# Two ties and a shorter step for the row products in a two-layer hybrid decoder trunk

## The chip, the cores and the metric

The kernel runs on one core of a Trainium2 chip. The metric is device time in microseconds (us), the median of three runs. TensorE (PE) multiplies matrices, VectorE (DVE) and ScalarE (ACT) work element by element, GpSimd (POOL) does a few tiny operations here, and the queue of SyncE (SP) issues the weight transfers.

## The reference

A sequence of 256 tokens of width 1024 passes two equal layers in fp32. In each layer `mod = silu(c) @ w_ada + b_ada` gives six vectors (shift, scale and gate of the mixer, shift, scale and gate of the MLP):

```
h = rms_norm(x, g_pre_mix) * (1 + sc_m) + sh_m
y = token_mixer(h)                 # MoBA and DSA attention, norms, out projection
x = x + gt_m * rms_norm(y, g_post_mix)
h = rms_norm(x, g_pre_ffn) * (1 + sc_f) + sh_f
a = causal_conv(h @ w_up_act)      # depthwise, width 3
y = (gelu(a) * (h @ w_up_lin)) @ w_down     # 2816 columns
x = x + gt_f * rms_norm(y, g_post_ffn)
```

## The kernel before

Tokens lie in two halves of 128 rows, t=0 and t=1. Each fp32 product is made of three fp32r products on PE: both operands are split into a high part, rounded, and a low part, the rest (`hh`/`hl` of activations, `wh`/`wl` or `dh`/`dl` of weights). A weight tile `raw` (1 MB, ring of 6 buffers, filled by the SP queue in program order) is split by `split`: ACT copies it to `wh` or `dh` (L141; L137 with a gain, in the out projection), DVE subtracts (L142, L138). `wh` and `wl` have rings of five buffers, `dh` and `dl` share a ring of six with other tiles.

The scale and gate vectors of the modulation are made on DVE: `gemv_v` multiplies a 128x1024 part of `w_ada` with the row `crow` and sums along it, one *row product* (L190), two per `raw` buffer. It is a generator: it runs beside the main work and yields, after each product, the number of steps after which it is traced again (`gap`). Columns 32 to 40 are the MLP scale, traced in attention with gap 9 in layer 0; columns 40 to 48 are the MLP gate, traced in the MLP loop from tile 3 (layer 0) or 7 (layer 1).

The program text gives each instruction a priority; a scheduler then sets the order of each engine's list from priorities, dependencies and its own estimates, so an instruction may move away from the place in which it was traced. `tc.issue_after(x)` ties an instruction: in the list it comes behind `x`. On the chip each engine works its list off.

The stages that the change touches, in order of time:

- Attention of layer 0: projections (L400), scores and value products (L420), masks and maxima of the scores on DVE (L484), exps on ACT (L488), scaling (L496), transposes (L503), copied by ACT (L505).
- Out projection (L576 to L578, `mm3`), then the *boundary*: residual (L319, L327), sums of squares on ACT (L255), the root on POOL (L263, L265), `norm_T` (L287: two tensor_scalar per half of the rows, then eight PE transposes, L275), and `mod_T`, which applies scale and shift and splits the result into `hh` and `hl` (L298, L306, L308 on ACT, L301, L310 on DVE).
- `lin`: the linear branch of the first four MLP tiles as one projection (L400) into banks b0 (t=0) and b1 (t=1). Its eight weight blocks k lie in four units; the units of k=0 to 5 are split into `dh`/`dl`, the last one (k=6, 7) into `wh`/`wl`. The first half of its result is copied (L940), transposed (L275) and copied again (L934).
- MLP: 22 column tiles; `up(i)` multiplies (L576 to L578, `hh` with `wh`), then conv on ACT and DVE (L968, L969, L971), gelu on ACT (L973), product with the linear branch (L974), and the split of the result into `ah` (L975, ACT) and `al` (L976, DVE); `down` multiplies these with `dh`/`dl` of `w_down` three tiles later (L576 to L578 with `dh`; its second product is the first that reads `al`).

Of the kernel before, what the change touches and what calls it, by code (L numbers as in the profile page):

```python
# [74 lines left out]
def trunk(ctx: ExitStack, tc, plan, x, c, stream, small, rope, out):  # L75
# [29 lines left out]

    st = {"off": 0, "behind": ()}

# [16 lines left out]
    def split(raw, where=None, pin=False, gain=None):  # L124
# [7 lines left out]
        with ExitStack() as behind:  # L132
            for ins in st["behind"]:
                behind.enter_context(tc.issue_after(ins))
            put = tc.keep_in_program_order if pin else lambda ins: ins
            if gain is not None:
                put(nc.scalar.activation(out=hi[:, :n], in_=raw, func=AF.Copy, scale=gain))  # L137
                put(nc.vector.scalar_tensor_tensor(out=lo[:, :n], in0=raw, scalar=gain, in1=hi[:, :n].bitcast(F32),  # L138
                                                   op0=OP.mult, op1=OP.subtract))
                return hi, lo  # L140
            put(nc.scalar.activation(out=hi[:, :n], in_=raw, func=AF.Copy))  # L141
            put(nc.vector.tensor_tensor(out=lo[:, :n], in0=raw, in1=hi[:, :n].bitcast(F32), op=OP.subtract))  # L142
        return hi, lo
# [39 lines left out]
    def gemv_v(l, j0, j1, gap, behind=None):  # L183

        for j in range(j0, j1, 2):
            r = load(("v_a", l, j, 2048))[0]
            for i in range(2):
                ri = r[:, 1024 * i:1024 * i + 1024]
                with tc.issue_after(behind) if behind else ExitStack():
                    nc.vector.scalar_tensor_tensor(out=ri, in0=ri, scalar=1.0, in1=crow, op0=OP.mult, op1=OP.mult,  # L190
# [93 lines left out]
    def norm_T(t, r, banks):  # L284
        xn = [t2(), t2()]
        for h in range(2):
            nc.vector.tensor_scalar(out=xn[h], in0=xt[:, t, 512 * h:512 * h + 512], scalar1=r, scalar2=None,  # L287
                                    op0=OP.mult)
        return [turn4(xn[h], banks[h]) for h in range(2)]
# [497 lines left out]
    for l in range(DEPTH):  # L787
# [83 lines left out]
        if l == 0:  # L871
            bg.add("sf", gemv_v(l, 32, 40, 9))
        run_project("dq", qk_done(dqT, True, "D", 10))
# [32 lines left out]
        while st["out"] < 2:  # L906
# [3 lines left out]
        out_load(4, 8)  # L910
        first = [[split(raw, "lin" if g < 1 or u < 1 else None) for u, raw in enumerate(load(*us))]
                 for g, us in enumerate(project_units(l, "lin"))]
        raws = []
# [73 lines left out]
        for i in range(NF):  # L987
            if i == 3 + 4 * l:
                bg.add("ada", gemv_v(l, 40, 48, 4))
                bg.add("ada", gate_rows(l, "ffn"))  # L990
# [97 lines left out]
```

## Time and profile before

| | us |
|---|---|
| median of three runs | 683.57 (683.51 to 684.01) |
| profiled execution | 685.16 |
| its span, first to last instruction | 683.4 |
| PE busy | 664.3 (97%) |
| DVE busy | 551.2 (81%) |
| ACT busy | 423.9 (62%) |
| POOL busy | 27.7 (4%) |
| mean granted clock of PE | 0.995 |

The profiled execution is one run, 1.6 us above the median; differences are read from it and set against the median. A busy share is a mean over stages; idle time of PE is what a change can win or lose, and idle time of the other engines counts where PE waits for them.

### The profile page before, as it was taken

The numbers are of one execution on the slowest core, as the hardware profiler recorded it, in microseconds if no ns is written. First come the engines' busy times: TensorE is split into PE (matmuls) and PEld (weight loads), VectorE is DVE, ScalarE is ACT, GpSimd is POOL, SyncE is SP. The second block draws the span as 40 slices with busy tenths as digits, with TensorE's granted clock in tenths as the row PEclk, the third lists the DMA queues.
The fourth block names the chain that finished last, engine by engine and source line by source line (L and its number), as shares of the span: only waits on it lengthen the run. The fifth ranks groups of instructions, "written<-read, shape, count | busy, mean of one in ns | idle before, by whom it ended". The sixth has DMA issues, their size and how long they took to land.

```text
span 683.4 us, 11282 instructions
## 1 busy us (share of the span) xinstructions
PE 664.3 (97%) x4309; PEld 570.0 (83%) x4309; DVE 551.2 (81%) x1090; ACT 423.9 (62%) x788; POOL 27.7 (4%) x56
## 2 busy tenths in 40 slices
PE   8999899998999999999999999999999999999996
PEld 5877677776999999999988776877799999999994
DVE  6899999977999999897689995677689976666553
ACT  6566686977855555555586548778595555555441
POOL 1000000102000000000020000001200000000001
PEclk9999999999999999999999999999999999999999
DMA  9999649953599999896537642446146885555001
GB/s 358 421 413 395 220 192 368 340 188 124 211 361 351 396 371 346 327 335 244 186 124 267 256 165 83 147 161 240 70 185 245 313 304 195 208 185 186 0 1 62
DMA packets 24806, 163.04 MB, mean 239 GB/s; under 512 B 3344, under 2 KB 3760, under 8 KB 6576
## 3 DMA queue, kind: packets, MB, share of 16 engines
q1 hardware_dynamic: 23472, 159.77, 62.0%
q0 software_dynamic: 704, 2.11, 1.1%
q8 instruction: 34, 0.56, 0.3%
q10 hardware_dynamic: 576, 0.43, 0.2%
q14 instruction: 20, 0.16, 0.1%
HBM read 161.24 MB, written 1.06 MB: 238 GB/s over the span
## 4 chain that ended last, share of the span: by engine, by line
PE 78%; DVE 10%; ACT 5%; issue 3%; DMA 2%; POOL 1%; POOLq 0%; DVEq 0%; ACTq 0%
PE b L578 18%; PE b L577 18%; PE b L576 18%; PE b L400 14%; DVE wl L142 3%; PE b L420 3%; DMA raw<-in_stream_dram 2%; DVE iscore L443 2%; PE b L503 2%; DVE raw L709 1%; ACT t L255 1%; PE b L377 1%; PE b L275 1%; ACT wh L137 1%; ACT t L488 1%
## 5 line engine op out<-in xcount | busy, mean ns | idle before, releaser
L142 DVE TENSOR_TENSOR wl<-raw,wh 128x1024 fp32r<-128x1024 f32 (+1 forms) x146 | 173.0, 1195 | 31.6 <-ACT wh L141 28.6
L141 ACT ACTIVATE wh<-raw 128x1024 fp32r<-128x1024 f32 (+1 forms) x146 | 149.2, 1045 | 52.3 <-PE b L578 37.6
L576 PE MATMUL b<-hh,wh 128*128 128x256 f32 x640 | 180.0, 281 | 0.0
L578 PE MATMUL b<-hl,wh 128*128 128x256 f32 x640 | 179.7, 281 | 0.0
L577 PE MATMUL b<-hh,wl 128*128 128x256 f32 x640 | 179.6, 281 | 0.0
L577 PEld LDWEIGHTS b<-hh,wl 128*128 128x128 f32 x640 | 122.5, 191 | 1.3
L576 PEld LDWEIGHTS b<-hh,wh 128*128 128x128 f32 x640 | 120.2, 188 | 1.4
L578 PEld LDWEIGHTS b<-hl,wh 128*128 128x128 f32 x640 | 120.1, 188 | 0.0
L190 DVE SCALAR_TENSOR_TENSOR raw<-raw,crow 128x1024 f32<-128x1024 f32 x72 | 86.6, 1216 | 0.8 <-DMA raw<-in_stream_dram 0.7
L400 PE MATMUL b<-wh,hh 128*128 128x512 f32 (+1 forms) x184 | 73.7, 402 | 0.2
L400 PE MATMUL b<-wh,hl 128*128 128x512 f32 (+1 forms) x184 | 69.2, 391 | 0.0
L142 DVE TENSOR_TENSOR dl<-raw,dh 128x1024 fp32r<-128x1024 f32 (+2 forms) x47 | 56.8, 1210 | 12.6 <-ACT dh L141 12.6
L141 ACT ACTIVATE dh<-raw 128x1024 fp32r<-128x1024 f32 (+2 forms) x47 | 49.5, 1058 | 26.6 <-PE b L577 26.6
L968 ACT ACTIVATE t<-b,smt 128x256 f32<-128x256 f32 x44 | 25.1, 571 | 57.3 <-PE b L578 57.3
L576 PE MATMUL b<-dh,t 128*128 128x512 f32 x152 | 59.7, 393 | 0.0
L577 PE MATMUL b<-dh,t 128*128 128x512 f32 x152 | 59.6, 392 | 0.0
L578 PE MATMUL b<-dl,t 128*128 128x512 f32 x152 | 59.1, 389 | 0.0
L400 PE MATMUL b<-wl,hh 128*128 128x512 f32 (+1 forms) x184 | 55.0, 392 | 0.0
L400 PEld LDWEIGHTS b<-wh,hh 128*128 128x128 f32 x184 | 34.8, 189 | 8.5 <-issue 1.5
L400 PEld LDWEIGHTS b<-wl,hh 128*128 128x128 f32 x184 | 34.3, 191 | 6.0 <-issue 0.2
L400 PEld LDWEIGHTS b<-wh,hl 128*128 128x128 f32 x184 | 34.0, 189 | 6.0 <-issue 0.5
L969 DVE SCALAR_TENSOR_TENSOR t<-b,smt,t 128x255 f32<-128x255 f32 x44 | 21.1, 480 | 21.0 <-ACT t L968 20.8
(172 smaller groups left out, 1101.5 us busy)
## 6 DMA issues: line engine op xcount, KB each, us to landing
raw<-in_stream_dram SPq DMA_DIRECT2D x142, 1024.0 KB, 6.5
raw<-in_stream_dram SPq DMA_DIRECT2D x7, 804.0 KB, 11.4
gate<-gated POOLq DMA_DIRECT2D x4, 512.0 KB, 8.7
raw<-in_stream_dram SPq DMA_DIRECT2D x3, 512.0 KB, 6.3
xt<-in_x_dram SPq DMA_DIRECT2D x2, 512.0 KB, 4.1
raw<-in_stream_dram SPq DMA_DIRECT2D x1, 984.0 KB, 5.0
out_dram<-xt SPq DMA_DIRECT2D x2, 256.0 KB, 2.1
raw<-in_stream_dram SPq DMA_DIRECT2D x1, 328.0 KB, 5.5
```

Source lines behind the costliest of these rows:

```text
L141: put(nc.scalar.activation(out=hi[:, :n], in_=raw, func=AF.Copy))
L142: put(nc.vector.tensor_tensor(out=lo[:, :n], in0=raw, in1=hi[:, :n].bitcast(F32), op=OP.subtract))
L190: nc.vector.scalar_tensor_tensor(out=ri, in0=ri, scalar=1.0, in1=crow, op0=OP.mult, op1=OP.mult, accum_out=mods[l][:, j + i:j + i + 1])
L400: mm = lambda l_, k, i, start=False, stop=False: nc.tensor.matmul(a[:, :n], lhsT=l_[:, k, tt], rhs=w[k][i], start=start, stop=stop)
L420: ins = nc.tensor.matmul(out, lhsT=lhsT, rhs=rhs, **flags)
L443: nc.vector.scalar_tensor_tensor(out=sc, in0=r[:, j * nk:j * nk + nk], scalar=wi[:, h:h + 1], in1=fill[:, 256 - nk:] if first else sc, op0 ...
L503: nc.tensor.transpose(tp[:, 128 * j:128 * j + 128], e[:, 128 * j:128 * j + 128], ident)
L576: nc.tensor.matmul(y, lhsT=hh, rhs=wh, start=first, stop=False)
L577: nc.tensor.matmul(y, lhsT=hl, rhs=wh, start=False, stop=False)
L578: nc.tensor.matmul(y, lhsT=hh, rhs=wl, start=False, stop=last)
L968: nc.scalar.activation(out=z, in_=p[:, :256], func=AF.Identity, scale=w2[:, i:i + 1], bias=bc[:, i:i + 1])
L969: nc.vector.scalar_tensor_tensor(out=z[:, 1:], in0=p[:, :255], scalar=w1[:, i:i + 1], in1=z[:, 1:], op0=OP.mult, op1=OP.add)
```

## The change

Three edits. The row products of columns 32 to 40 are traced in layer 0 with gap 6, not 9. In layer 0 the split of lin's last unit (k=6, 7) is no longer made with the other units; it is put on a list, and `norm_T` of t=1 makes it, tied behind its second tensor_scalar. The gate products (columns 40 to 48, both layers) are each tied behind the lo split that was traced last. The number of instructions on each engine stays.

```
@@ -103,7 +103,7 @@
         return wrk.tile([128, n], F32, name=f"tiny{n}", tag=f"tiny{n}", bufs=8)
 
 
-    st = {"off": 0, "behind": ()}
+    st = {"off": 0, "behind": (), "then": []}
 
     def load(*units, cut=None):
 
@@ -139,7 +139,8 @@
                                                    op0=OP.mult, op1=OP.subtract))
                 return hi, lo
             put(nc.scalar.activation(out=hi[:, :n], in_=raw, func=AF.Copy))
-            put(nc.vector.tensor_tensor(out=lo[:, :n], in0=raw, in1=hi[:, :n].bitcast(F32), op=OP.subtract))
+            d = put(nc.vector.tensor_tensor(out=lo[:, :n], in0=raw, in1=hi[:, :n].bitcast(F32), op=OP.subtract))
+            st["lo"] = d.ins
         return hi, lo
 
 
@@ -186,7 +187,8 @@
             r = load(("v_a", l, j, 2048))[0]
             for i in range(2):
                 ri = r[:, 1024 * i:1024 * i + 1024]
-                with tc.issue_after(behind) if behind else ExitStack():
+                after = st["lo"] if behind == "lo" else behind
+                with tc.issue_after(after) if after else ExitStack():
                     nc.vector.scalar_tensor_tensor(out=ri, in0=ri, scalar=1.0, in1=crow, op0=OP.mult, op1=OP.mult,
                                                    accum_out=mods[l][:, j + i:j + i + 1])
                 yield gap
@@ -284,8 +286,11 @@
     def norm_T(t, r, banks):
         xn = [t2(), t2()]
         for h in range(2):
-            nc.vector.tensor_scalar(out=xn[h], in0=xt[:, t, 512 * h:512 * h + 512], scalar1=r, scalar2=None,
-                                    op0=OP.mult)
+            d = nc.vector.tensor_scalar(out=xn[h], in0=xt[:, t, 512 * h:512 * h + 512], scalar1=r, scalar2=None,
+                                        op0=OP.mult)
+        if t and st["then"]:
+            with tc.issue_after(d.ins):
+                st["then"].pop()()
         return [turn4(xn[h], banks[h]) for h in range(2)]
 
     def mod_T(p, t, scale, bias, hh, hl, between=None):
@@ -869,7 +874,7 @@
         bg.add("att", attend(mqT, mkT, mv, None, 0, oh, ol, ready[0]))
         dqT, dkT, dv = big("qT"), big("kT"), big("v")
         if l == 0:
-            bg.add("sf", gemv_v(l, 32, 40, 9))
+            bg.add("sf", gemv_v(l, 32, 40, 6))
         run_project("dq", qk_done(dqT, True, "D", 10))
         run_project("dk", qk_done(dkT, False, "D", 7))
         bg.add("att", attend(dqT, dkT, dv, masks, 4, oh, ol, ready[1]))
@@ -908,8 +913,14 @@
         bg.run(out_first(range(3)))
         bg.drain("att", "out")
         out_load(4, 8)
-        first = [[split(raw, "lin" if g < 1 or u < 1 else None) for u, raw in enumerate(load(*us))]
-                 for g, us in enumerate(project_units(l, "lin"))]
+        first = [load(*us) for us in project_units(l, "lin")]
+        first[0] = [split(raw, "lin") for raw in first[0]]
+        first[1][0] = split(first[1][0], "lin")
+        if l:
+            first[1][1] = split(first[1][1])
+        else:
+
+            st["then"].append(lambda: first[1].append(split(first[1].pop())))
         raws = []
         bg.run(out_last(range(3, 8)))
         bg.drain("sf")
@@ -986,7 +997,7 @@
 
         for i in range(NF):
             if i == 3 + 4 * l:
-                bg.add("ada", gemv_v(l, 40, 48, 4))
+                bg.add("ada", gemv_v(l, 40, 48, 4, "lo"))
                 bg.add("ada", gate_rows(l, "ffn"))
                 if l + 1 < DEPTH:
                     bg.add("ada", gemv_v(l + 1, 0, 32, 5))
```

Line numbers of the new kernel are higher: L190 becomes L192, L275 L277, L287 L289, L301 L306, L310 L315, L327 L332, L400 L405, L420 L425, L484 L489, L488 L493, L496 L501, L505 L510, L569 L574, L576 to L578 L581 to L583, L940 L945, L969, L971, L974, L976 become L980, L982, L985, L987.

What moves in the lists is shown at three places; the number behind a name tells buffers apart. First PE in layer 0's boundary, from the last `hh` products of lin's t=0 half on; `b0` is the bank of t=0, `b1` that of t=1, `b6` and `b4` take the transposes of t=1. Before:

```order
L400 MATMUL b0_1882<-wh_1694,hh_1762 128x512
L400 MATMUL b0_1882<-wl_1695,hh_1762 128x512
L400 MATMUL b0_1882<-dh_1680,hl_1763 128x512 x2
L400 MATMUL b0_1882<-dh_1684,hl_1763 128x512
L275 MATMUL b6_1849<-ident_75,t2_1845 128x128 x4
L275 MATMUL b4_1854<-ident_75,t2_1846 128x128 x4
L400 MATMUL b0_1882<-dh_1684,hl_1763 128x512
L400 MATMUL b0_1882<-dh_1690,hl_1763 128x512 x2
L400 MATMUL b0_1882<-wh_1694,hl_1763 128x512 x2
L400 MATMUL b1_1909<-dh_1680,hh_1762 128x512
```

Now:

```order
L405 MATMUL b0_1882<-dh_1692,hh_1758 128x512
L405 MATMUL b0_1882<-dl_1693,hh_1758 128x512
L405 MATMUL b0_1882<-wh_1845,hh_1758 128x512
L277 MATMUL b6_1849<-ident_75,t2_1841 128x128 x4
L277 MATMUL b4_1854<-ident_75,t2_1842 128x128 x4
L405 MATMUL b1_1909<-dh_1684,hh_1758 128x512
L405 MATMUL b1_1909<-dl_1685,hh_1758 128x512
L405 MATMUL b1_1909<-dh_1684,hh_1758 128x512
L405 MATMUL b0_1882<-wl_1846,hh_1758 128x512
L405 MATMUL b0_1882<-wh_1845,hh_1758 128x512
L405 MATMUL b0_1882<-wl_1846,hh_1758 128x512
```

The pair of the last unit (`wh_1694`, `wl_1695` before, `wh_1845`, `wl_1846` now) keeps one product ahead of the transposes; its other three, and the `hl` products, stand behind the transposes and behind three products of t=1.

Next DVE at the first MLP tile of layer 0, from the sixth split on; `t2_1987` is tile 0's conv result, `t2_1988` holds its `ah` and `al`. Before:

```order
L142 TENSOR_TENSOR dl_2072<-raw_2039,dh_2071 128x1024
L969 SCALAR_TENSOR_TENSOR t2_1987<-b5_1943,smt_71,t2_1987 128x255
L971 SCALAR_TENSOR_TENSOR t2_1987<-b5_1943,smt_71,t2_1987 128x254
L142 TENSOR_TENSOR wl_2098<-raw_2041,wh_2097 128x1024
L974 TENSOR_TENSOR t2_1987<-lin_1880,t2_1987 128x256
L142 TENSOR_TENSOR wl_2162<-raw_2155,wh_2161 128x1024
L976 TENSOR_TENSOR t2_1988<-t2_1987,t2_1988 128x256
```

Now:

```order
L142 TENSOR_TENSOR dl_2072<-raw_2039,dh_2071 128x1024
L142 TENSOR_TENSOR wl_2098<-raw_2041,wh_2097 128x1024
L192 SCALAR_TENSOR_TENSOR raw_2107,mod0_98<-raw_2107,crow_107 128x1024
L980 SCALAR_TENSOR_TENSOR t2_1987<-b5_1943,smt_71,t2_1987 128x255
L142 TENSOR_TENSOR wl_2162<-raw_2155,wh_2161 128x1024
L982 SCALAR_TENSOR_TENSOR t2_1987<-b5_1943,smt_71,t2_1987 128x254
L142 TENSOR_TENSOR wl_2193<-raw_2155,wh_2192 128x1024
L985 TENSOR_TENSOR t2_1987<-lin_1880,t2_1987 128x256
L142 TENSOR_TENSOR wl_2251<-raw_2157,wh_2250 128x1024
L987 TENSOR_TENSOR t2_1988<-t2_1987,t2_1988 128x256
```

A row product (of a buffer whose two products stood in the boundary before) and two more splits, `wl_2193` and `wl_2251`, stand ahead of tile 0's last operation. On ACT `wh_2192` and `wh_2250` stand ahead of tile 0's gelu now; before, the gelu was ahead of both.

Last ACT in attention, behind the exps (L488) of the first group of heads; the copies `t2_1422`, `t2_1432` (now `t2_1426`, `t2_1436`) are what the value products read. Before:

```order
L488 ACTIVATE t2_1392,tiny4_1397<-t2_1392,tiny4_1391 128x128 x4
L137 ACTIVATE wh_1503<-raw_1497,smt_71 128x1024
L137 ACTIVATE wh_1602<-raw_1600,smt_71 128x1024
L505 ACTIVATE t2_1422<-b7_1417 128x512
L137 ACTIVATE wh_1606<-raw_1600,smt_71 128x1024
L505 ACTIVATE t2_1432<-b6_1427 128x512
```

Now:

```order
L493 ACTIVATE t2_1396,tiny4_1401<-t2_1396,tiny4_1395 128x128 x4
L137 ACTIVATE wh_1507<-raw_1501,smt_71 128x1024
L137 ACTIVATE wh_1607<-raw_1605,smt_71 128x1024
L137 ACTIVATE wh_1611<-raw_1605,smt_71 128x1024
L510 ACTIVATE t2_1426<-b7_1421 128x512
L510 ACTIVATE t2_1436<-b6_1431 128x512
```

The third `wh` split went ahead of the first copy.

## Rows read from the trace of the kernel before

In the rows of the timeline the columns are: start in us, duration in us, engine, line, operation, out<-in, partitions x elements and type, count; in brackets the idle time ahead and who ended it.

**Rows 1.** The page's first part: busy time, share of the span and number of instructions of each engine.

```profile
PE 664.3 (97%) x4309; PEld 570.0 (83%) x4309; DVE 551.2 (81%) x1090; ACT 423.9 (62%) x788; POOL 27.7 (4%) x56
```

**Rows 2.** Timeline of PE in layer 0's boundary, from the last out product to the first up product.

```profile
157.44 0.40 PE L578 MATMUL b<-wl,hh 128*128 128x512 f32 x1
158.65 1.09 PE L275 MATMUL b<-ident,t 128*128 128x128 f32 x8 [0.81 <-DVE t L287]
159.85 0.50 PE L400 MATMUL b<-dh,hh 128*128 128x512 f32 x1
...
163.73 0.40 PE L400 MATMUL b<-wl,hh 128*128 128x512 f32 x1
...
164.43 0.85 PE L400 MATMUL b<-dh,hl 128*128 128x512 f32 x3
165.61 1.11 PE L275 MATMUL b<-ident,t 128*128 128x128 f32 x8 [0.32 <-DVE t L287]
166.48 0.94 PE L400 MATMUL b<-dh,hl 128*128 128x512 f32 x3
...
173.68 0.28 PE L576 MATMUL b<-hh,wh 128*128 128x256 f32 x1
```

**Rows 3.** Timeline of DVE in the same stretch.

```profile
154.09 1.22 DVE L190 SCALAR_TENSOR_TENSOR raw<-raw,crow 128x1024 f32<-128x1024 f32 x1
...
155.24 1.22 DVE L190 SCALAR_TENSOR_TENSOR raw<-raw,crow 128x1024 f32<-128x1024 f32 x1
...
156.99 1.21 DVE L142 TENSOR_TENSOR wl<-raw,wh 128x1024 fp32r<-128x1024 f32 x1
158.12 0.87 DVE L287 TENSOR_SCALAR t<-xt,tiny 128x512 f32<-128x512 f32 x2
...
165.06 0.88 DVE L287 TENSOR_SCALAR t<-xt,tiny 128x512 f32<-128x512 f32 x2 [0.97 <-POOL tiny L265]
```

**Rows 4.** Timeline of PE in layer 1's boundary, from the last out product to the transposes of t=1.

```profile
487.48 0.40 PE L578 MATMUL b<-wl,hh 128*128 128x512 f32 x1
487.71 1.19 PE L275 MATMUL b<-ident,t 128*128 128x128 f32 x8
489.00 0.50 PE L400 MATMUL b<-dh,hh 128*128 128x512 f32 x1
...
494.76 1.11 PE L275 MATMUL b<-ident,t 128*128 128x128 f32 x8 [0.34 <-DVE t L287]
```

**Rows 5.** Timeline of DVE in the same stretch of layer 1: the split that stands between the two tensor_scalar of t=0.

```profile
486.57 1.22 DVE L142 TENSOR_TENSOR wl<-raw,wh 128x1024 fp32r<-128x1024 f32 x1
```

**Rows 6.** Timelines at the first MLP tile of layer 0: DVE from the end of the six splits to `al` of tile 0, then the first two down products of PE.

```profile
178.30 0.48 DVE L969 SCALAR_TENSOR_TENSOR t<-b,smt,t 128x255 f32<-128x255 f32 x1
178.81 0.48 DVE L971 SCALAR_TENSOR_TENSOR t<-b,smt,t 128x254 f32<-128x254 f32 x1
179.21 1.22 DVE L142 TENSOR_TENSOR wl<-raw,wh 128x1024 fp32r<-128x1024 f32 x1
180.34 0.42 DVE L974 TENSOR_TENSOR t<-lin,t 128x256 f32<-128x256 f32 x1
...
181.81 0.42 DVE L976 TENSOR_TENSOR t<-t,t 128x256 fp32r<-128x256 f32 x1
...
182.60 0.40 PE L576 MATMUL b<-dh,t 128*128 128x512 f32 x1
182.83 0.40 PE L577 MATMUL b<-dh,t 128*128 128x512 f32 x1
```

**Rows 7.** Timelines in layer 0's attention: DVE, then ACT, then PE.

```profile
114.27 1.21 DVE L142 TENSOR_TENSOR wl<-raw,wh 128x1024 fp32r<-128x1024 f32 x1
115.40 0.68 DVE L569 TENSOR_TENSOR o<-o,b 128x512 f32<-128x512 f32 x1
...
120.32 0.28 DVE L484 CUSTOM_DVE_ANT_0 t<-b,mask 128x128 f32<-128x128 f32 x1
...
122.34 0.18 DVE L491 RECIPROCAL rs<-tiny 128x4 f32<-128x4 f32 x1 [0.24 <-ACT t L488]
...
120.67 0.38 ACT L488 ACTIVATE t<-t,tiny 128x128 f32<-128x128 f32 x1
...
123.76 2.17 ACT L137 ACTIVATE wh<-raw,smt 128x1024 fp32r<-128x1024 f32 x2
...
127.35 0.57 ACT L505 ACTIVATE t<-b 128x512 f32<-128x512 f32 x1
...
116.73 0.39 PE L400 MATMUL b<-wl,hh 128*128 128x512 f32 x1
...
127.98 1.09 PE L420 MATMUL b<-t,v 128*64 128x128 f32 x16 [0.20 <-ACT t L505]
```

**Rows 8.** Busy time by stretch: from and to, length, then PE, PEld, DVE, ACT and POOL with the number of instructions, granted clock of PE, DMA share and GB/s.

```profile
80.00:83.00 3.00, 1.81 (x11) 1.15 (x12) 3.00 (x15) 2.24 (x11) 0.00 (x0) 0.96 0.20 33
83.00:86.00 3.00, 3.00 (x12) 2.60 (x11) 3.00 (x11) 1.56 (x3) 0.00 (x0) 0.50 0.80 314
...
158.00:161.00 3.00, 2.24 (x13) 1.83 (x14) 2.81 (x8) 2.21 (x7) 1.06 (x2) 1.00 0.98 358
161.00:164.00 3.00, 2.50 (x12) 1.71 (x11) 2.67 (x5) 2.99 (x9) 0.00 (x0) 1.00 0.70 276
164.00:167.00 3.00, 2.68 (x16) 2.02 (x15) 1.22 (x4) 0.70 (x2) 0.86 (x2) 1.00 0.07 27
```

More of the change, by code (lines that the diff above doesn't have):

```diff
@@ L103, in tiny @@
         return wrk.tile([128, n], F32, name=f"tiny{n}", tag=f"tiny{n}", bufs=8)
-    st = {"off": 0, "behind": ()}
+    st = {"off": 0, "behind": (), "then": []}
     def load(*units, cut=None):
@@ L141, in split @@
             put(nc.scalar.activation(out=hi[:, :n], in_=raw, func=AF.Copy))
-            put(nc.vector.tensor_tensor(out=lo[:, :n], in0=raw, in1=hi[:, :n].bitcast(F32), op=OP.subtract))
+            d = put(nc.vector.tensor_tensor(out=lo[:, :n], in0=raw, in1=hi[:, :n].bitcast(F32), op=OP.subtract))
+            st["lo"] = d.ins
         return hi, lo
@@ L188, in gemv_v @@
                 ri = r[:, 1024 * i:1024 * i + 1024]
-                with tc.issue_after(behind) if behind else ExitStack():
+                after = st["lo"] if behind == "lo" else behind
+                with tc.issue_after(after) if after else ExitStack():
                     nc.vector.scalar_tensor_tensor(out=ri, in0=ri, scalar=1.0, in1=crow, op0=OP.mult, op1=OP.mult,
@@ L286, in norm_T @@
         for h in range(2):
-            nc.vector.tensor_scalar(out=xn[h], in0=xt[:, t, 512 * h:512 * h + 512], scalar1=r, scalar2=None,
-                                    op0=OP.mult)
+            d = nc.vector.tensor_scalar(out=xn[h], in0=xt[:, t, 512 * h:512 * h + 512], scalar1=r, scalar2=None,
+                                        op0=OP.mult)
+        if t and st["then"]:
+            with tc.issue_after(d.ins):
+                st["then"].pop()()
         return [turn4(xn[h], banks[h]) for h in range(2)]
@@ L871, in trunk @@
         if l == 0:
-            bg.add("sf", gemv_v(l, 32, 40, 9))
+            bg.add("sf", gemv_v(l, 32, 40, 6))
         run_project("dq", qk_done(dqT, True, "D", 10))
@@ L910, in trunk @@
         out_load(4, 8)
-        first = [[split(raw, "lin" if g < 1 or u < 1 else None) for u, raw in enumerate(load(*us))]
-                 for g, us in enumerate(project_units(l, "lin"))]
+        first = [load(*us) for us in project_units(l, "lin")]
+        first[0] = [split(raw, "lin") for raw in first[0]]
+        first[1][0] = split(first[1][0], "lin")
+        if l:
+            first[1][1] = split(first[1][1])
+        else:
+            st["then"].append(lambda: first[1].append(split(first[1].pop())))
         raws = []
@@ L988, in trunk @@
             if i == 3 + 4 * l:
-                bg.add("ada", gemv_v(l, 40, 48, 4))
+                bg.add("ada", gemv_v(l, 40, 48, 4, "lo"))
                 bg.add("ada", gate_rows(l, "ffn"))
```

## The prediction

> **What bounds the kernel now.** I read the busy shares first: TensorE (PE) is busy 97% of the span, DVE 81% [rows 1]. So only what makes PE wait, or takes a wait of PE away, can move the time; DVE's own length does not matter, its order does. Then I looked for the places where PE waits beside the edits: the boundary of layer 0 between the out projection and the MLP, the first MLP tile behind it, and the attention stage in which the MLP-scale products run.
>
> In layer 0's boundary the last out matmul starts at 157.44, the transposes of the first half of the rows (t=0) at 158.65 after 0.81 us of idle for DVE's `t` of L287, the lin product (L400) at 159.85; PE waits 0.32 for the transposes of t=1 (165.61), and the first up tile starts at 173.68 [rows 2]. DVE shows why the first wait is there: two MLP-gate row products (L190, at 154.09 and 155.24) and one lo split (L142, at 156.99) stand ahead of L287 at 158.12 [rows 3]. Layer 1's boundary has no row products there: its transposes start at 487.71, 0.23 after the last out matmul at 487.48, without idle, and L400 at 489.00 [rows 4].
>
> **The change, part by part.** Sums are made against the profiled execution (685.16 us) and carried to the median of the three runs, 683.57; differences, not totals, are carried.
>
> *Products out of the boundary (the "lo" tie).* In the new order the two products are gone from it, and the lo split too. As in layer 1 the transposes then follow the last out matmul: 157.44 + 0.23 = 157.67. From there to L400 layer 1 takes 1.29, so L400 starts at 158.96, not at 159.85: a gain of 0.89. Bounds: 0 (something else is late there) and 0.98 (the whole of 158.65 − 157.67).
>
> *The split moved behind the tensor_scalar of t=1.* It is no cost on DVE, which idles 0.97 ahead of that tensor_scalar [rows 3]; but its `wl` is now ready only after the t=1 transposes could start, and the list order of PE followed it: three products with that pair and three `hl` products, which stood ahead of the t=1 transposes, stand behind them. The transposes of t=1 hang on a chain over DVE, ACT and POOL that starts with t=0's `hh` and takes 5.76 from the first L400 in both layers (165.61 − 159.85, 494.76 − 489.00) [rows 2, 4]; it does not get shorter, so they start at 158.96 + 5.76 = 164.72. PE runs out of work earlier: at 163.73 it began the fourteenth product [rows 2], 3.88 after the first, so now at 162.84, and it idles 1.88. Six products of 0.23 us (163.73 to 164.43 is three of them), 1.40, come later that ran in this gap before. Behind the transposes stand now products that need t=1's `hh`; from transposes to first L400 it took 1.20 (158.65 to 159.85), the eight transposes take 0.87 (165.61 to 166.48): 0.33 more. Up tile 0 starts at 173.68 − 0.89 + 1.40 + 0.33 = 174.52, **0.84 later**.
>
> The place rests on PE keeping the order of its queue. The rows say so: at 165.29 PE waited 0.32 for the transposes while five `hl` products that read the same finished `hl` stood behind them and did not start [rows 2]. The Trainium skill ("TensorE: Matmul & The Clock Gate", Part 3, The mechanism) says that matmuls start and end strictly in order, while its Part 1 (Architectural detail) tells of a partial reorder window that pulls weight loads ahead. If that window let products pass a waiting transpose, the 1.40 and 0.33 would fall away; by the first rule and by the trace they stay.
>
> *The first tile's chain on DVE.* Down of tile 0 starts at 182.60, and its second product, which needs `al` (L976), at 182.83; L976 starts at 181.81 and takes 0.42: the margin is 0.60 [rows 6]. In the new order four splits and a row product (not two splits) stand between the sixth split and L976 (L987 in the new numbers), and the gelu on ACT stands behind a `wh` split that waits for a buffer that PE frees with up tile 1. Their steps from the rows: split 1.14 (156.99 to 158.12), row product 1.15 (154.09 to 155.24), L969 and L971 0.40 each (178.81 to 179.21), L974 and L976 0.42 each [rows 3, 6]. Start: the sixth split's `dh` stands on ACT behind the copy of the second lin half, whose last product ends with the start of up tile 0, 174.5 and its own 0.4; copy 0.5 and `dh` 1.1, as the copies and splits of [rows 7], and `dl` 1.15: DVE is free at about 177.6 (178.30 before [rows 6]). Then 177.6 + 1.14 + 1.15 + 0.40 + 1.14 + 0.40 + 1.14 + 0.42 + 1.13 + 0.42 = 184.9. PE wants it at 182.83 + 0.84 = 183.67: **it waits 1.2 us**. Bounds: 0 (DVE's order costs nothing, PE's delay covers it) and 1.8 (another 0.6 if the load for a third product, whose buffer is freed only by one of these splits, holds tile 1 too). I take 1.2. Note that the two terms stand in for one another: what counts is the later of PE and `al`, so even if PE lost nothing, `al` at about 184 would hold down of tile 0 by more than 1 us. Later tiles have growing margins, which I count as cover.
>
> *Products every sixth step.* In layer 0's attention the same eight products run, but one more of them now stands ahead of the value projection's splits. DVE is full there (no idle in its rows ahead of the 0.24 at 122.34); its fourth split starts at 114.27, PE reads its result at 116.73 [rows 7]: margin 1.25. In the new order that split is 1.15 (product) + 0.60 (L569, also ahead of it now) later: a wait of up to 0.5, which the next figure holds within it. Behind it two products instead of one and a half stand ahead of the masks-and-max operations (L484), which by the same adding start 1.1 later than 120.32. ACT's eight exps, which took 120.67 to 123.76, end at 124.9. Then, new too, three `wh` splits of 1.04 (not two, a copy and one) go ahead of both copies L505: 124.9 + 3.1 + 0.5 + 0.6 = 129.1 for the second copy, on which PE's value products (L420, 127.98 [rows 7]) wait. PE has one more product of 0.23 ahead of them now: **0.9 later**. Bounds: −0.2 (today's stall of 0.20 there gone) and 1.1.
>
> *Layer 1's gate products* are tied too, in the middle of the MLP. What hides them is the distance that splits keep there ahead of PE; they cost nothing. If that cover were gone, one product is 1.2.
>
> Sum: 0.84 + 1.2 + 0.9 = 2.9; 683.57 + 2.9 = **686.5** (profiled: 688.1).
>
> **Rivals.**
> *A: one of the three is covered.* PE's loss and the wait for `al` are 2.06 together, the attention term 0.9. Without attention 685.6; without the wait for `al` 685.3. For it: ACT could slip ahead where a transfer or semaphore lets it; against it: order on each engine is fixed. 0.18.
> *B: two are covered.* For instance the attention term is zero and `al` comes in time: 684.4. 0.11.
> *C, the other side: the boundary becomes layer 1's.* If the t=1 chain starts earlier because DVE is free of 1.2 us of split ahead of `L301`, its 5.76 shrinks. Layer 1 is against it: there the split lies between the two L287 [rows 5] and yet the chain is as long as in layer 0, so DVE does not set it. The 1.40 and 0.33 vanish only if L287 of t=1 starts 1.7 earlier than 164.2, before 162.5, and `al` must then be there by 181.9: then 0.89 is kept, 682.7. 0.05, and 0.03 that the bounds' gain in attention comes with it, 682.5 or less.
> *D: the clock falls.* PE's granted clock is 0.50 in 83 to 86, behind a stretch in which PE was busy only 1.81 of 3.00; in 161 to 164 and 164 to 167 it is busy 2.50 and 2.68, and keeps 1.00 [rows 8]. The new order takes 1.7 more out of these six microseconds. If the clock falls to its lower level, 1.2 GHz, for 3 us as there, lin's second half ends 1.5 later and `al` with it: 688.0. Against it: the rows of 158 to 167 hold 1.6 us of idle at full clock. 0.10. The Trainium skill (same page, Part 1, HAM oscillation) says of kernels with waits between short runs of matmuls that they fall to half clock again and again; by that rule D would be nearer than I take it.
> That the change does nothing: the lists differ on PE, DVE and ACT, so this case, 683.6, is counted in B.
>
> **How the numbers follow.** Main forecast 0.53 (its own range 685.8 to 687.2), A 0.18, B 0.11, C 0.08, D 0.10. The range from 684.2 to 687.6 leaves out D, C and some of B, about 2 in 10. A measurement tells 0.2% or 1.37 us from no change: slower starts at 684.94, faster below 682.20. Slower: main, A and D, less their tails, 0.77; within: B, most of C, the tails, 0.19; faster 0.04.
>
> **What would show it.** Boundary: PE's transposes 0.2 behind the last out matmul, L400 1.2 to 1.3 later; then one idle of some 1.9 ahead of the t=1 transposes and 0.3 behind them; up tile 0 about 17.1 after the last out matmul (16.24 before). First tile: an idle of PE of 1 to 1.3 for DVE's L987 at the second down product. Attention: an idle of about 1.2 ahead of the value products, for ACT's L510. The forecast is wrong if PE's idle at the t=1 transposes is under 1, if down of tile 0 starts without a wait, or if the clock row shows a second dip.

## The result and the profile after

| | before | after |
|---|---|---|
| median, us | 683.51 (683.35 to 684.01) | **687.44** (686.16 to 688.13) |
| ratio to before | | 1.0053, 95% interval 1.0039 to 1.0067 |
| profiled execution, us | 685.16 | 686.27 |
| its span | 683.4 | 684.5 |

The change made the kernel slower by 0.53%. The executions of both kernels differ by the granted clock of PE: the execution profiled before had 3 us at the lower level (in 83 to 86, [rows 8]) and its 685.16 is 1.6 above the usual 683.5; the execution profiled after has none, and three others of it are 1.2 to 1.9 above it. So 686.3 against 683.5, **+2.8**, is what the order of the work costs in an execution at the full clock, and the rest of the median, **1.1**, is the clock. Both are followed below.

First the page's busy shares of the changed kernel: PE's work is the same as in [rows 1], less what the lower clock stretched there.

```profile
PE 661.9 (97%) x4309; PEld 567.8 (83%) x4309; DVE 551.4 (81%) x1090; ACT 423.7 (62%) x788; POOL 27.6 (4%) x56
```

PE's waits in the changed kernel (us in total, times, longest): the first, fifth and seventh row are new or longer; before they read 2.0 (longest 0.8) for the tensor_scalar, nothing, and 0.4 (0.2).

```profile
PE b L277 <- DVE t L289: 2.5, 3, 1.7
...
PE b L581 <- ACT wh L141: 1.2, 1, 1.2
...
PE b L425 <- ACT t L510: 1.0, 2, 0.8
```

Timeline of PE in layer 0's boundary, with DVE's last operation on `hl` of t=0 as the last line (start, duration, engine, line, operation, out<-in, shape, count, idle ahead and who ended it), to be set against [rows 2]:

```profile
156.39 0.40 PE L583 MATMUL b<-wl,hh 128*128 128x512 f32 x1
156.62 1.03 PE L277 MATMUL b<-ident,t 128*128 128x128 f32 x8
157.91 0.50 PE L405 MATMUL b<-dh,hh 128*128 128x512 f32 x1 [0.25 <-ACT hh L303]
...
161.56 0.40 PE L405 MATMUL b<-wh,hh 128*128 128x512 f32 x1
163.66 1.11 PE L277 MATMUL b<-ident,t 128*128 128x128 f32 x8 [1.71 <-DVE t L289]
164.87 0.50 PE L405 MATMUL b<-dh,hh 128*128 128x512 f32 x1
...
173.45 0.28 PE L581 MATMUL b<-hh,wh 128*128 128x256 f32 x1
...
160.85 1.29 DVE L315 TENSOR_TENSOR hl<-t,hh 128x512 fp32r<-128x512 f32 x2
```

The transposes of t=0 follow the last out product at once, as forecast; then PE stands 1.71 us ahead of those of t=1. Up tile 0 starts 17.06 after the last out product (173.45 − 156.39); before it was 16.24 (173.68 − 157.44).

Timelines of PE and DVE at the first MLP tile, against [rows 6]:

```profile
179.34 0.28 PE L583 MATMUL b<-hl,wh 128*128 128x256 f32 x1
180.80 0.36 PE L581 MATMUL b<-hh,wh 128*128 128x256 f32 x1 [1.19 <-ACT wh L141]
...
183.60 0.40 PE L581 MATMUL b<-dh,t 128*128 128x512 f32 x1
183.84 0.40 PE L582 MATMUL b<-dh,t 128*128 128x512 f32 x1
...
178.65 0.48 DVE L980 SCALAR_TENSOR_TENSOR t<-b,smt,t 128x255 f32<-128x255 f32 x1
179.05 1.21 DVE L142 TENSOR_TENSOR wl<-raw,wh 128x1024 fp32r<-128x1024 f32 x1
180.18 0.47 DVE L982 SCALAR_TENSOR_TENSOR t<-b,smt,t 128x254 f32<-128x254 f32 x1
...
183.18 0.42 DVE L987 TENSOR_TENSOR t<-t,t 128x256 fp32r<-128x256 f32 x1
```

From up tile 0 to the first down product it is 10.15 (183.60 − 173.45), before 8.92 (182.60 − 173.68): +1.23. But the wait is not where I put it. The down products start without one, `al` (L987) being done at 183.60, 0.24 ahead of its first reader at 183.84. PE waits at 180.80 for up tile 2. The trace names ACT's `wh` (L141); that split is one for a later tile, and in PE's list tile 2 writes bank b5, the bank of tile 0, which DVE's L982 reads last (180.18 + 0.47 = 180.65). So I read it as a bank that is given back late; that is tested below.

In attention the value products stand behind 0.80 of idle (0.20 in [rows 7]; the times there are some 1.6 later, since the clock had fallen ahead of them):

```profile
122.97 3.22 ACT L137 ACTIVATE wh<-raw,smt 128x1024 fp32r<-128x1024 f32 x3
126.09 1.05 ACT L510 ACTIVATE t<-b 128x512 f32<-128x512 f32 x2
...
127.19 0.99 PE L425 MATMUL b<-t,v 128*64 128x128 f32 x14 [0.80 <-ACT t L510]
```

0.82 + 1.23 + 0.60 = 2.65, and 683.5 + 2.65 = 686.2: the executions without a clock stretch (686.2, 686.3) are accounted for.

### The profile page after: what moved, and what is told of

It is laid out like the page before. It is cut to its first block, busy times and chain, and to the rows that moved or that the text cites. A ratio compares the mean times of both kernels' runs of the same rounds, so it can differ in the third digit from the quotient of the medians.

```text
span 684.5 us, 11288 instructions
## 1 busy us (share of the span) xinstructions
PE 661.9 (97%) x4309; PEld 567.8 (83%) x4309; DVE 551.4 (81%) x1090; ACT 423.7 (62%) x788; POOL 27.6 (4%) x56
## 4 chain that ended last, share of the span: by engine, by line
PE 72%; DVE 14%; ACT 5%; issue 3%; DMA 3%; POOL 1%; SPq 0%; POOLq 0%; DVEq 0%; ACTq 0%
PE b L583 19%; PE b L581 19%; PE b L582 18%; PE b L405 11%; DVE wl L142 4%; DMA raw<-in_stream_dram 3%; PE b L425 2%; DVE iscore L448 2%; DVE raw L714 1%; DVE raw L192 1%; DVE iscore L460 1%; ACT t L257 1%; PE b L508 1%; DVE tiny L459 1%; DVE t L489 1%
## 5 line engine op out<-in xcount | busy, mean ns | idle before, releaser
L141 ACT ACTIVATE wh<-raw 128x1024 fp32r<-128x1024 f32 (+1 forms) x146 | 148.7, 1042 | 52.6 <-PE b L583 37.0
L581 PE MATMUL b<-hh,wh 128*128 128x256 f32 x640 | 180.0, 281 | 1.2 <-ACT wh L141 1.2
L583 PE MATMUL b<-hl,wh 128*128 128x256 f32 x640 | 179.6, 281 | 0.0
L581 PEld LDWEIGHTS b<-hh,wh 128*128 128x128 f32 x640 | 120.2, 188 | 2.8 <-ACT wh L141 1.4
L583 PEld LDWEIGHTS b<-hl,wh 128*128 128x128 f32 x640 | 120.1, 188 | 0.0
L192 DVE SCALAR_TENSOR_TENSOR raw<-raw,crow 128x1024 f32<-128x1024 f32 x72 | 86.8, 1217 | 0.0
L405 PE MATMUL b<-wh,hh 128*128 128x512 f32 (+1 forms) x184 | 73.0, 399 | 0.2
L405 PE MATMUL b<-wh,hl 128*128 128x512 f32 (+1 forms) x184 | 69.1, 390 | 0.0
L141 ACT ACTIVATE dh<-raw 128x1024 fp32r<-128x1024 f32 (+2 forms) x47 | 49.5, 1057 | 25.7 <-PE b L582 25.7
L581 PE MATMUL b<-dh,t 128*128 128x512 f32 x152 | 59.7, 393 | 0.0
L583 PE MATMUL b<-dl,t 128*128 128x512 f32 x152 | 59.2, 389 | 0.0
L405 PE MATMUL b<-wl,hh 128*128 128x512 f32 (+1 forms) x184 | 54.9, 390 | 0.0
L405 PEld LDWEIGHTS b<-wh,hh 128*128 128x128 f32 x184 | 34.6, 188 | 8.6 <-issue 1.5
L405 PEld LDWEIGHTS b<-wl,hh 128*128 128x128 f32 x184 | 33.9, 189 | 5.8 <-issue 0.2
L405 PEld LDWEIGHTS b<-wh,hl 128*128 128x128 f32 x184 | 33.9, 189 | 5.8 <-issue 0.5
L980 DVE SCALAR_TENSOR_TENSOR t<-b,smt,t 128x255 f32<-128x255 f32 x44 | 21.1, 480 | 17.9 <-ACT t L979 17.8
```

The costliest lines, as they stand in the source:

```text
L405: mm = lambda l_, k, i, start=False, stop=False: nc.tensor.matmul(a[:, :n], lhsT=l_[:, k, tt], rhs=w[k][i], start=start, stop=stop)
L581: nc.tensor.matmul(y, lhsT=hh, rhs=wh, start=first, stop=False)
L583: nc.tensor.matmul(y, lhsT=hh, rhs=wl, start=False, stop=last)
L980: nc.vector.scalar_tensor_tensor(out=z[:, 1:], in0=p[:, :255], scalar=w1[:, i:i + 1], in1=z[:, 1:], op0=OP.mult, op1=OP.add)
```

## The experiments

### Each edit alone

The *lo tie* puts the gate products behind the lo split that was traced last. Alone, with the split of lin's last unit and the gap as before:

```
-                bg.add("ada", gemv_v(l, 40, 48, 4))
+                bg.add("ada", gemv_v(l, 40, 48, 4, "lo"))
```

> Only the tie of the gate products to the latest lo split (both layers). Theory 1: layer 0's boundary becomes as long as layer 1's: transposes 0.2 after the last out product, six products still ahead of the transposes of t=1, idle there 0.3; up tile 0 at 15.4 after the last out product (16.24 before); no new wait at the first tile; 0.9 faster, 682.6. Rival: the products that come later hold the first tile (al or a bank), and the gain is given back: 683.5 or more.

Measured 682.70 (682.36 to 683.09), ratio 0.9982 (0.9974 to 0.9991): faster than both kernels. PE in its boundary:

```profile
155.96 0.40 PE L583 MATMUL b<-wl,hh 128*128 128x512 f32 x1
156.19 1.10 PE L277 MATMUL b<-ident,t 128*128 128x128 f32 x8
...
163.24 1.12 PE L277 MATMUL b<-ident,t 128*128 128x128 f32 x8 [0.31 <-DVE t L289]
...
171.31 0.28 PE L581 MATMUL b<-hh,wh 128*128 128x256 f32 x1
```

171.31 − 155.96 = 15.35, against 16.24: the gain of 0.89 of the forecast to the hundredth, and the list order behind it is that of before. Against the changed kernel (17.06) it is 1.71 shorter; the forecast had 1.40 + 0.33 = 1.73 for the products that the second tie puts behind the wait.

The *second tie* puts the split of lin's last unit behind the tensor_scalar of t=1. Alone, with gap 9 and no lo tie:

```
-                bg.add("ada", gemv_v(l, 40, 48, 4, "lo"))
+                bg.add("ada", gemv_v(l, 40, 48, 4))
...
-            bg.add("sf", gemv_v(l, 32, 40, 6))
+            bg.add("sf", gemv_v(l, 32, 40, 9))
```

> Only the last lin split behind the tensor_scalar of t=1, in layer 0. Theory 1: the two row products stay in the boundary but no longer hold the t=0 transposes (their split has gone from ahead of them): gain 0.8; idle of PE ahead of the t=1 transposes 1.7 to 1.9, loss 1.4 and 0.3; at the first tile three splits stand ahead of the second conv step, up tile 2 waits 1.3 for its bank: 685.7. Rival (the loss comes from the gate products, not from the split): 683.5 to 684.4 and no wait at up tile 2.

Measured 685.93 (685.85 to 687.43), ratio 1.0035 (1.0022 to 1.0048). PE in its boundary and at up tile 2:

```profile
156.00 0.39 PE L583 MATMUL b<-wl,hh 128*128 128x512 f32 x1
156.23 1.09 PE L277 MATMUL b<-ident,t 128*128 128x128 f32 x8
...
163.27 1.12 PE L277 MATMUL b<-ident,t 128*128 128x128 f32 x8 [1.71 <-DVE t L289]
...
173.05 0.28 PE L581 MATMUL b<-hh,wh 128*128 128x256 f32 x1
...
180.44 0.36 PE L581 MATMUL b<-hh,wh 128*128 128x256 f32 x1 [1.22 <-ACT wh L141]
```

Both waits are there in full (1.71 at the transposes of t=1, 1.22 at up tile 2). Its boundary takes 17.05 from the last out product (156.00) to up tile 0 (173.05), as with both ties, although the row products are still in it: with the split gone from ahead of the tensor_scalar, the transposes of t=0 follow the last out product at once (156.23). What held them up before was the split alone, not the products. So the 0.89 is to be had by either tie, once, and all the loss of boundary and first tile comes with the second.

The gap alone:

```
-            bg.add("sf", gemv_v(l, 32, 40, 9))
+            bg.add("sf", gemv_v(l, 32, 40, 6))
```

> Only the MLP-scale products every sixth step. Theory 1: ACT's third split stands ahead of both copies, PE waits 0.8 for the second copy ahead of the value products (0.2 before); the rest as before: 0.6 slower, 684.1. Rival: the attention stage gives it back later, or the earlier products shorten the boundary: 683.5 or less.

Measured 684.26 (683.94 to 685.41), ratio 1.0008 (0.9999 to 1.0017), 0.7 above the 683.55 beside it; the idle ahead of the value products is 0.81. The interval just touches 1; the trace carries the reading.

The lo tie in layer 1 only:

```
-                bg.add("ada", gemv_v(l, 40, 48, 4, "lo"))
+                bg.add("ada", gemv_v(l, 40, 48, 4, "lo" if l else None))
```

> The kernel before with the lo tie on the gate products of layer 1 alone. Prediction's step: they cost nothing, since the splits there keep a distance ahead of PE. Theory: 683.5, no difference, and so the gain of the lo tie alone (0.85) is layer 0's boundary. Rival: part of that gain is layer 1's: 683.1 or below. Rival: the cover is missing and a tied product delays a split there: 684.7.

Measured 683.65 against 683.60, ratio 1.0001 (0.9992 to 1.0009): nothing, as forecast.

### The same split, tied one half earlier

```
-        if t and st["then"]:
+        if not t and st["then"]:
```

> The changed kernel, with the split of lin's last unit tied behind the second tensor_scalar of t=0 and not of t=1. It is still moved out from ahead of the transposes of t=0, but the list of PE is that of the kernel before again (four products with the pair and three hl products ahead of the transposes of t=1), and DVE's list at the first tile has L980 and L982 ahead of the splits again. Theory (the later `wl` cost time only by the two lists that the scheduler made of it, 0.8 and 1.2 us with the 0.9 that the boundary gained taken off): 682.7 of the lo tie alone + 0.6 of the sixth step = 683.3, waits ahead of the t=1 transposes under 0.6 and none ahead of up tile 2. Rival (taking the split out from ahead of t=0's tensor_scalar by any tie holds DVE up at `mod_T` of t=0, so that the chain to t=1 is 1.2 longer): 684.5. Rival (the first tile is late for the row products of the gate, not for the split): 684.5, with the wait ahead of up tile 2.

Measured 683.17 (682.90 to 684.82), ratio 0.9999 (0.9990 to 1.0007). PE in its boundary:

```profile
162.45 0.84 PE L405 MATMUL b<-dh,hl 128*128 128x512 f32 x3
163.62 1.11 PE L277 MATMUL b<-ident,t 128*128 128x128 f32 x8 [0.33 <-DVE t L289]
164.49 0.94 PE L405 MATMUL b<-dh,hl 128*128 128x512 f32 x3
...
171.73 0.28 PE L581 MATMUL b<-hh,wh 128*128 128x256 f32 x1
```

The wait of 1.71 is 0.33 again, no wait stands at up tile 2, and down of tile 0 starts 8.72 behind up tile 0 (180.45); up tile 0 comes 15.38 after the last out product (156.35). What cost the time is thus not that the split moved from its place, but that behind t=1 its result came after the transposes, and the scheduler put six products there and reordered DVE's list at the first tile. What is left, 683.17 − 682.70 = 0.5, is the gap.

### Whose wait is it at up tile 2?

```
-            p = bank(4 + (i + 1) % 2)
+            p = bank((5, 4, 7)[i % 3] if not l and i < 6 else 4 + (i + 1) % 2)
```

> The changed kernel, but the up products of the first six tiles of layer 0 go round three PSUM banks (b5, b4, b7) and not two, so that up tile 2 no longer takes the bank of tile 0. Theory (the 1.3 us in front of up tile 2 are for bank b5, which DVE reads last in L982 of tile 0, late because a row product and two splits stand ahead of it): the wait in front of up tile 2 is gone. PE then reaches down of tile 0 at 182.4 instead of 183.6; `al` of tile 0 is ready at 183.60 as before, its first reader is the second down product, so a wait of about 1.0 for DVE's L987 appears there, the one that the prediction named: 686.0 to 686.3 in executions at the full clock (the changed kernel: 686.3). Rival 1 (the profile's own name, ACT's `wh` by L141, holds up tile 2): the wait of 1.2 stays in front of up tile 2. Rival 2 (`al` is not late by itself and would not hold PE): wait gone and none takes its place, 685.0.

PE, DVE and ACT of this kernel:

```profile
179.01 0.28 PE L583 MATMUL b<-hl,wh 128*128 128x256 f32 x1
179.12 0.28 PE L581 MATMUL b<-hh,wh 128*128 128x256 f32 x1
...
182.18 0.28 PE L581 MATMUL b<-hh,wh 128*128 128x256 f32 x1
182.64 1.20 PE L581 MATMUL b<-dh,t 128*128 128x512 f32 x4 [0.18 <-ACT t L986]
183.68 0.28 PE L582 MATMUL b<-hh,wl 128*128 128x256 f32 x1
183.79 0.40 PE L582 MATMUL b<-dh,t 128*128 128x512 f32 x1
...
180.19 0.48 DVE L982 SCALAR_TENSOR_TENSOR t<-b,smt,t 128x254 f32<-128x254 f32 x1
...
183.19 0.42 DVE L987 TENSOR_TENSOR t<-t,t 128x256 fp32r<-128x256 f32 x1
...
179.66 1.07 ACT L141 ACTIVATE wh<-raw 128x1024 fp32r<-128x1024 f32 x1 [0.61 <-PE b L583]
```

ACT's `wh` and DVE's L982 stand where they stood (179.66 and 180.19), and PE goes through tile 2 without a wait: it was the bank, not the split that the trace names (L982 is the last of the three operations that read it). PE reaches the first down product 0.96 earlier (182.64). My expectation of a new wait of 1.0 for `al` failed: `al` is as late as before (183.61), but the scheduler put five products that don't need it (four with `dh` and `ah`, one of up) ahead of its first reader, which starts at 183.79. In the changed kernel's list that reader is the second product; here it would have come at 182.9 and waited some 0.7. That list was not run. Four of the five executions have a clock of 0.996 or less and 687.0 to 687.9, so the median is 687.29 (ratio 1.0051, 1.0038 to 1.0064), no better than the changed kernel's; the one at 0.998, the profiled one, has 685.38, 0.9 below the changed kernel's 686.3. What the bank is worth in time thus rests on one execution; that the wait is gone is in its trace. The Trainium skill ("Perfetto Trace Analysis", Optimizing Tensor Performance, Matmuls) advises rotating independent groups of matmuls through different PSUM banks, so that reading one out overlaps the next; here a third bank brought PE to the first down product 0.96 earlier, because the reader of the first bank was late.

### The clock

The changed kernel once more:

> The changed kernel once more, to see why its five times lie between 686.2 and 688.1. Theory 1 (clock): the profile that was taken has no half-clock stretch and belongs to the lower times; executions with a mean clock of 0.995 to 0.996 are 1.3 to 1.9 us longer than those with 0.998 or 0.999, and if this run's profile is one of them it shows PE at half clock for about 3 us, either at 82 (as the kernel before's profile) or behind the new idle at 161 to 164 (rival D of the prediction). Theory 2: the spread is of waits (loads, tile 1); then clock and time are not related, and the longer profile shows another wait of PE of over 1 us.

Measured 687.35 (686.30 to 687.92), ratio 1.0044 (1.0031 to 1.0056). The profiled execution was one of the longer ones (span 685.6). Busy time by stretch (columns as in [rows 8]), first the changed kernel's first profile, then this one:

```profile
161.00:164.00 3.00, 1.29 (x8) 0.77 (x7) 2.03 (x5) 1.04 (x4) 0.86 (x2) 1.00 0.00 0
164.00:167.00 3.00, 2.91 (x16) 2.27 (x15) 2.42 (x6) 2.64 (x8) 0.00 (x0) 1.00 0.28 44
```

```profile
161.00:164.00 3.00, 1.29 (x7) 0.77 (x6) 2.03 (x5) 1.04 (x4) 0.86 (x2) 0.89 0.00 0
164.00:167.00 3.00, 3.00 (x13) 2.59 (x12) 2.46 (x6) 2.18 (x7) 0.00 (x0) 0.54 0.27 44
167.00:170.00 3.00, 3.00 (x15) 2.44 (x14) 2.11 (x4) 2.62 (x6) 0.00 (x0) 1.00 0.75 311
```

and from its timeline:

```profile
174.56 0.28 PE L581 MATMUL b<-hh,wh 128*128 128x256 f32 x1
```

With the same 1.29 us of work in 161 to 164 the clock stayed at 2.4 GHz once and went to 1.2 GHz once, for the products behind the idle. Up tile 0 starts at 174.56, not at 173.45: 1.1 later. That is the rival D of the forecast, at its place. The stretch of [rows 8] in which the clock fell in the profile before keeps the full clock here (1.00 in 83 to 86).

To test whether the idle brings it, ten products that nobody reads were put into the gap:

```
         p = bank(b)
+        if fill:
+            for _ in range(10):
+                nc.tensor.matmul(p[:, 0:256], lhsT=fill[1][:, 7, 0:128], rhs=fill[0][:, 6:8, 0:128], start=True, stop=True)
```

> The changed kernel with ten more products on PE, 128x256 each, whose result nobody reads (they go into bank b6, which the transposes of t=1 overwrite), in the list just ahead of the transposes of t=1: they read the last hl of t=0, ready at about 162.1, and take some 1.2 us, so they end before the transposes' data at 163.6. They add work but no delay. Theory (in part of the executions the granted clock falls to its lower level behind PE's idle stretch at 161.6 to 163.7, as in the second look at the changed kernel, and that costs 1.1): with the gap filled no execution has it here; all five runs at 686.2 to 686.4 (of ten plain executions of the changed kernel six were at 687.3 to 688.1). Rival (the fall of the clock has nothing to do with this gap): half the runs again at 687.3 to 688.1, and the median 686.9 or more. Rival (the ten products are late themselves): all runs at 687 with the transposes later than 163.7.

> The kernel with the filled gap once more (ten products of 128x256 in front of the transposes of t=1, read by nobody), for a second profile and five more executions. Theory (the idle gap brings the fall of the granted clock): in most executions 686.7 to 687.0, as four of the first five; falls no more frequent than in kernels without the gap (13 of 91 executions so far). Rival (the gap has nothing to do with it): about 3 of 5 at 687.8 or more, as in the kernels with the gap (12 of 20 executions had it).

Measured 686.80 (686.72 to 688.24; ratio 1.0053, 1.0039 to 1.0066) and 686.76 (686.58 to 687.23; 1.0046, 1.0033 to 1.0058). PE's timeline in the gap (lines of this kernel are five higher), and its busy time there with the granted clock, 1.00:

```profile
162.38 1.45 PE L278 MATMUL b<-hh,hl 128*128 128x256 f32 x10 [0.23 <-DVE hl L319]
163.84 1.12 PE L280 MATMUL b<-ident,t 128*128 128x128 f32 x8
165.37 0.50 PE L410 MATMUL b<-wl,hh 128*128 128x512 f32 x1 [0.41 <-DVE wl L142]
```

```profile
161.00:164.00 3.00, 2.76 (x16) 1.98 (x16) 2.02 (x5) 1.22 (x5) 0.86 (x2) 1.00 0.00 0
```

They end as the transposes can start: these come 7.27 after the last out product (156.57), as in the changed kernel (163.66 − 156.39). The expectation of 686.2 to 686.4 failed by 0.4. Of it 0.31 stands between the last out product and up tile 0 (17.37 against 17.06), behind the wait of 0.41: in this list a product with the late `wl` came first, which I had not seen. One of ten executions is 1.5 above the shortest ones (688.24, clock 0.996); it was not profiled.

In kernels with the open gap (changed, changed again, second tie alone, third bank) 12 of 20 executions were 1.0 or more above the kernel's shortest ones, and those 12, no others, had a mean clock of 0.996 or less. In kernels without it (63 executions of the kernel before, 66 of six others) 16 of 129 had a clock of 0.995 or 0.996. The wait at up tile 2 could have been the cause as well, as it came with the same edit. The runs speak against it: the filled kernel has that wait (1.2) and one such execution in ten, the third bank takes it away and has four in five.

Most executions of the changed kernel had the lower clock, few of the filled one. So the filled kernel's median is 0.6 lower, although its execution at the full clock is 0.4 longer; the ratios of the two kernels overlap, so that 0.6 is not a shown gain. Where in the program the clock fell is seen in profiled executions only, for the gap in one. That the gap makes falls more frequent is shown by these counts. Why the clock falls in one execution and not in the next is open, and so is why the third bank's executions with the lower clock are 1.7 to 2.5 above its other one, against 1.0 to 1.9 in the changed kernel.

### The gap in the other direction

```
-            bg.add("sf", gemv_v(l, 32, 40, 9))
+            bg.add("sf", gemv_v(l, 32, 40, 10))
```

and the same with 12, both with the lo tie alone.

> The lo tie alone, and the MLP-scale row products of layer 0 every tenth step instead of every ninth. In ACT's list a copy L510 of the value products' input now stands between the `wh` splits, so the stall of 0.2 to 0.4 in front of the value products could go. Theory (what counts in attention is what stands ahead of ACT's copies): 682.3 to 682.5, against 682.7 of the lo tie alone. Rival (DVE's maxima of the scores come in time anyway, and the copies wait for PE): 682.7. Rival (the later row products reach the out projection and delay splits there): 683.5 or more.

> The lo tie alone with a step of 12 between the MLP-scale row products of layer 0. By the first theory of the run with a step of ten: 682.3 to 682.5. More of the products stand late, so if the third possibility of that run (late products delay splits of the out projection) is real it shows here first: 683.5 or more.

Measured 682.74 (0.9986, 0.9977 to 0.9995) and 682.62 (0.9984, 0.9975 to 0.9992): the same as 682.70 with gap 9. With gap 10 the copies are indeed earlier and the value products start 0.68 earlier than in the lo tie alone (125.73 against 126.41), but with four products fewer ahead of them and 0.27 of idle still there:

```profile
125.73 1.09 PE L425 MATMUL b<-t,v 128*64 128x128 f32 x16 [0.27 <-ACT t L510]
...
131.79 0.35 PE L563 MATMUL b<-mean,ss 128*128 128x1 f32 x2 [0.25 <-DVE ss L536]
```

and a wait for DVE that was hidden before comes up at 131.79. The first theory falls: an earlier start of one operation is no gain if PE only took its work in another order. The lo tie without the second tie is the fastest form that was measured, with no difference between the gaps 9, 10 and 12.

## Why the prediction was right, and where it was not

The forecast was 686.5 (684.2 to 687.6), slower with 0.77; measured 687.44. The sign and the range held, the range partly by luck: the main forecast's own range ended at 687.2, and the median is an execution in which the clock had fallen, the rival D that had 0.10 and was left out of the range. Two of the five executions (688.00 and 688.13) lie beyond 687.6. By its steps:

- **Products out of the boundary:** 0.89 forecast, 0.89 measured (15.35 against 16.24 with the lo tie alone). Layer 1's rows, as the pattern for layer 0, were the right source. I had named the products and the split as what holds the transposes of t=0; by the second tie alone it is the split.
- **The split behind t=1:** 17.08 from the last out product to up tile 0 forecast (16.24 + 0.84), 17.06 measured. The idle of 1.88 is 163.66 − 161.56 − 0.23 = 1.87 from start to start (the trace counts 1.71, from the modelled end of the product). PE held to the order of its list: `hl` of t=0 was ready at 162.14 (DVE's L315, 160.85 and 1.29 long), and the `hl` products stood behind the waiting transposes all the same.
- **The first tile:** size 1.2 forecast, 1.23 measured; the mechanism was wrong. I followed `al` to the second down product. The same row product and splits ahead of tile 0's operations on DVE make L982 late first, and L982 gives back the bank that up tile 2 needs, 2.8 us of PE's work earlier. The forecast named a down tile that starts without a wait as a sign against it, and that is what the trace shows. That the sizes agree to 0.03 is luck. `al` is ready 10.15 after up tile 0 (183.60 − 173.45) and would have been wanted at 9.15 (182.83 − 173.68), so in this list it would have cost 1.0 by itself; the bank cost 1.2, and `al` is then covered with 0.24 to spare. Both are late from the same cause, DVE's order. I had listed what DVE's operations make, but not what they free.
- **Products every sixth step:** 0.9 forecast; 0.6 by the idle, 0.4 to 0.7 by the runs (0.4 from the second tie alone, 685.9, to the changed kernel, 686.3, both at the full clock; 0.5 from the lo tie alone to the split tied behind t=0; 0.7 by the gap alone). The place and the cause (three `wh` splits ahead of both copies) are right; the size is not, because I took the later start of the value products as the loss, though one product more had been done ahead of them; only the growth of the idle (0.80 − 0.20) is lost.
- **Layer 1's gate products:** nothing forecast, nothing measured.
- **The clock (rival D, 0.10 and 1.5):** its price was 1.1 in the profiled execution, and it came in 12 of 20 executions of kernels with the gap. The forecast named a second dip of the clock as a sign against it. I weighed it by two stretches of 3 us that had kept the full clock with more work in them [rows 8]; the new stretch had 1.29, less than the 1.81 behind which the clock had fallen in the very rows I quoted, and even so kept the full clock in one profile and lost it in the other. The Trainium skill ("TensorE: Matmul & The Clock Gate", Part 1, A second HAM failure mode: psum-queue depth-cycling) tells of a kernel in which frequent short idle spells of PE between groups of matmuls sent it back and forth between its levels; the runs agree that a short spell can do it, here a single one of 1.7. The section that the forecast names (HAM oscillation) tells of waits for DMA longer than that, so it is not the one that bears on this gap.

So the median is 2.65 to 2.8 (2.9 forecast) of work in a worse order and 1.1 of clock, which the sum had left out. Without the clock the forecast would have been 0.2 high; with it, it is 0.9 low. Rivals A and B (terms that are covered) did not come: each of the three terms is in the trace. C did not, either: the chain to t=1 took 5.75 (163.66 − 157.91), as before.

## What to carry to other kernels

When instructions are moved on an engine, follow what each of them frees (a PSUM bank, a buffer) as well as what it makes: the bank was wanted a tile earlier than the result, and the trace's name for that wait was another instruction that ended at about the same time. A tie that puts a producer behind a late event moves its readers in the other engine's list too; here the same split tied half a boundary earlier brought none of the waits. And an idle stretch of PE can cost more than its own length, by the clock, and in some executions only: one profiled execution is not enough to rule that out, and two medians may differ by how many of their executions had the lower clock.

## What the runs showed of the hardware

The operation of POOL that starts the root (L263, L265 in the new numbers) took five times as long when DVE was in row products. Before, and in the changed kernel:

```profile
155.03 1.51 POOL L263 TENSOR_SCALAR tiny<-tiny 128x1 f32<-128x1 f32 x1 [2.30 <-ACT t L255]
```

```profile
153.98 0.30 POOL L265 TENSOR_SCALAR tiny<-tiny 128x1 f32<-128x1 f32 x1 [2.31 <-ACT t L257]
```

It also took 1.51 with the second tie alone, where the row products are still there, and 0.30 with the lo tie alone. The one of before ends at 156.54, 0.08 after the row product that started at 155.24 [rows 3]. The Trainium skill ("SBUF — State Buffer", SBUF: two separate sides) says that DVE and GpSimd share a pair of ports as an exclusive lock, which a DVE operation with two SBUF inputs takes for its whole length against a GpSimd operation that reads SBUF; the trace agrees. It is no part of the first wait of [rows 2]: the root was ready all the same at 157.18, 0.94 ahead of the tensor_scalar at 158.12, which stood behind the split.

```profile
156.62 0.56 POOL L265 TENSOR_TENSOR tiny<-tiny,mhalf 128x1 f32<-128x1 f32 x1
```

With the second tie alone POOL's operation was as long, and PE did not wait.

One execution of the filled kernel and one of the kernel before had a mean granted clock of 0.947 and were 0.5 to 0.9 above their medians. The filled one was profiled: the clock is 0.95 from end to end, yet its products in the boundary start 0.23 apart as in the other profiles. Another execution of that kernel was as long (687.23) at 0.998, so that the clock cost the 0.5 is not shown; no run here shows the cause of the 0.947.
